# A hybrid encoder trunk on one core: the first projections of layer 0 rebuilt (value projection in the loop over input tiles, shift and scale side by side, one sine chain for all angles)

## The chip, the core and the metric

The kernel runs on 1 core of one Trainium2 chip. The metric is device time in microseconds. Three runs of the kernel before took 1063.59 to 1066.42 us; the median is 1063.81 us. The core has a matrix engine (TensorE, PE in the profile; its weight loads are PEld), a vector engine (VectorE, DVE), a scalar engine (ScalarE, ACT), GpSimd (POOL) and SyncE (SP), which issues the DMA transfers of this kernel. Each engine works through its own list of instructions in order; waits between engines go by semaphores.

## The reference, cut to what matters

Two layers, 256 tokens, 1024 channels. Only the first sub-layer of layer 0 is touched, so only its head is shown.

```
cond = silu(c)
for l in range(2):
    mod = cond @ w_ada[l] + b_ada[l]                  # 1024 -> 6 * 1024
    shift1, scale1, gate1, shift2, scale2, gate2 = split(mod, 6)
    h = layer_norm(x) * (1 + scale1) + shift1
    proj = h @ w_in[l]
    q_c, kv_c, k_r, r_q, r_k, r_v, r_g, s5_u, gates = split(proj, ...)
    #  256   128   32  256  256  512  512  512   3072  columns
    o_mla = mla(q_c, kv_c, k_r, positions, ...)       # rope: cos, sin(positions * 10000**(-i/16))
    o_ret = retention(r_q, r_k, r_v, r_g, positions, log_decay)   # rope with 32 angles,
    #                                                 log_gamma = log1p(-exp(log_decay))
    o_s5 = s5(s5_u, ...)  # step = exp(log_step); a = exp(lam_re*step) * (cos, sin)(lam_im*step);
    #                       x_t = a x_(t-1) + B u_t, forward and backward, 32 groups x 64 states
    x = post_norm(alpha * x + gate1 * (sigmoid(gates) merge of the three @ w_o))
    ...                                               # conv FFN with shift2, scale2, gate2
```

## The kernel before, in words

Every operation goes through a recorder: the Python code records instructions in program order (a helper on one line issues them all, so the profile shows L736 for every row, and rows are told apart by tile names). `Recorder.schedule` (line 554) then simulates the engines with a table of costs and latencies and lists the instructions anew: on each engine the ready one with the lowest number of record goes first, moved by a bias and by a small random jitter with a fixed seed, if the pool has a place for its tiles. The pools are 37 places of 128x1024 f32 (weights, x, h and most other tiles), 9 and 18 smaller ones, and 8 banks of PSUM.

Weights come as tiles `raw` of 512 KB in the order of `_plan`, DMAs on SyncE. Each is split into `hi` (a cast to fp32r on ACT) and `lo` (raw minus hi, on DVE), and a product is three matmuls: hi with the activation's high part hh, lo with hh, and hi with the activation's low part hlo. Activations h are kept transposed, 8 tiles of 128 channels by 256 tokens.

`mixer` (line 1422) computes layer 0's first sub-layer. Its first part is a loop over k = 0, 2, 4, 6, two channel tiles a round. A round has: `ada_chunk` for the chunk of shift1 and then that of scale1 which belong to these 256 channels (each: two loads `ada0`, 8 matmuls 32x256 into a PSUM tile ada_ps, a copy z, two transposes, a reduction and an addition on DVE); `put_h`, which transposes the normalised x and applies scale and shift; `gemm_t` for b0 (q_c, kv_c and k_r, 416 columns) and for b1 (r_q and r_k, 512 columns), both accumulating in PSUM over all four rounds. The tile names b0, b1, b2 are one group "b" in the profile.

Behind the loop `rope_tables` (line 979) makes the cosine and sine of 352 columns in one chain of DVE instructions (`sincos`, line 924; tiles t): 96 columns for two token tiles (tokens on partitions), and 256 for the table qtab, whose angles stand on partitions and come from posf_i, the positions loaded to all 128 partitions. `prephase` (line 997) makes exp(log_step) and exp(log_decay) (tiles arena), the decays lg and nlg (16 columns, some 45 instructions), a second `sincos` of 64 columns, the powers pw, the factors fri, and by seven squarings the steps rot8. Then `s5.prep` (bbt) and `s5.rot` (tiles rot and g) build the tables of the S5 stage. kr is the first product of k_r with a rope table, and so the first use of the finished b0. uF is the S5 input; it is transposed in 32x32 blocks into uT0 and by two copies into uT.

b2 (r_v, 512 columns, 48 matmuls) is computed after the up-projection `ukv` of the latent. Then the S5 stage follows: `states` transposes tables into w_ps (tile w1), DVE makes scans X, results R are written to DRAM (rd) and read back as T, and PE multiplies T with U into Y.

Of the kernel before, what the change touches and what calls it, by code (L numbers as in the profile page):

```python
# [18 lines left out]
L = 2  # L19
# [47 lines left out]
def _plan(layer):  # L67
# [28 lines left out]
    if layer == 0:  # L96
        for k in range(0, 8, 2):
            block_t("b0_", "w_in", 0, 416, 2, [k])
            block_t("b1_", "w_in", 416, 928, 2, [k])
        block_f("u", "w_in", 1952, 4)  # L100
    else:
        block_t("b0_", "w_in", 0, 416, 2)
        block_f("u", "w_in", 1952, 4)
        block_t("b1_", "w_in", 416, 928, 2)
    for g in range(2):
        out.append((f"uq{g}", 1024, lambda w, l, g=g: uq(w, l, g)))
    out.append(("ukv", 1024, ukv))
    block_t("b2_", "w_in", 928, 1440, 2)
    names = ("w_branch_mla", "w_branch_ret", "w_branch_s5")
# [39 lines left out]

def ada_rows(l, c):  # L150

    return (l, c // 4) not in ((0, 0), (0, 1))


def _ada(w, l, key):
    c, k = (int(v) for v in key[3:].split("_"))
    if ada_rows(l, c):
        k += 2 * (c % 4)
        return w["w_ada"][l][k * P:(k + 1) * P, c // 4 * D:(c // 4 + 1) * D]
    return _rows(w["w_ada"][l][k * 512:(k + 1) * 512, c * 256:(c + 1) * 256]).reshape(P, -1)  # L160

# [22 lines left out]
def _small_layout():  # L184
    off, o = {}, 0
    for name, n in (("c", 8), ("lam_re", 64), ("lam_im", 64), ("log_step", 64), ("ret_ld", 16),
                    ("kv_norm", L), ("q_norm", 2 * L), ("conv_w", L * NFF * 2 * 3), ("conv_b", L * NFF * 2),
                    ("b_ada", L * 32), ("d", L * 8), ("freq_t", 48), ("freq_f", 1), ("sign_f", 1),
                    ("i16", 16)):
        off[name] = (o, o + n)  # L190
        o += n
    return off, o


def _host(w):
# [34 lines left out]
    put("freq_t", np.broadcast_to(np.concatenate([fr, fm])[None], (P, 48)))  # L230
    put("freq_f", np.concatenate([np.zeros(64, f32), fm, fm, fm, fm]))
    put("sign_f", np.concatenate([np.ones(96, f32), -np.ones(16, f32), np.ones(16, f32)]))
    i16 = np.tile(np.concatenate([np.eye(16, dtype=f32), np.zeros((16, 16), f32)]), (4, 1))
    put("i16", i16)

    def bc(a):
# [12 lines left out]
        "x": w["x"].reshape(2, P, D),  # L249
        "pos": w["positions"].reshape(1, S),  # L250
        "post": w["positions"].reshape(2, P).T,
# [488 lines left out]
def build(tc, A, dbg=None):  # L740
# [237 lines left out]

    def rope_tables():
        w = []  # L980
        for i in range(5):
            w2 = t4([P, 1024], f"t{i}")
            w += [w2[:, 0:352], w2[:, 512:864]]
        ang, sn, cs = w[6:9]
# [12 lines left out]
    def prephase():  # L997
        main[0] = V if PRE0 == 'V' else G

        ex = pre(80)  # L1000
        exi = pre(80)
        V.tensor_copy(exi[:, 0:64], sm("log_step"))
        V.tensor_copy(exi[:, 64:80], sm("ret_ld"))
        exp_acc(ex, exi, 80)
        step = ex[:, 0:64]
        e = ex[:, 64:80]

        q = [pre(16) for i in range(9)]
        y1, kx, m1, sel, nsel, num, den, z_, z2 = q
        ts(y1, e, -1.0, ALU.mult, 1.0, ALU.add)  # L1010
# [28 lines left out]

        main[0] = PRE[0]  # L1040
# [5 lines left out]
        main[0] = PRE[1]  # L1046

# [27 lines left out]
        for n in (1, 2, 4):  # L1075
# [3 lines left out]
                 br, bi, pt[0][:, :, 0:n], pt[1][:, :, 0:n])  # L1079
        main[0] = PRE[2]  # L1080
        V.tensor_copy(w[0], c_s)
        V.tensor_copy(w[1], s_s)
        for i in range(7):
            tt(w[2], w[0], w[0], ALU.mult)
            tt(w[3], w[1], w[1], ALU.mult)
            tt(w[4], w[0], w[1], ALU.mult)
            dst = (w[0], w[1]) if i < 2 else (rot8[:, i - 2, 0], rot8[:, i - 2, 1])
            if i >= 2:
                tt(dst[0], w[2], w[3], ALU.subtract)
                ts(dst[1], w[4], 2.0, ALU.mult)  # L1090
                V.tensor_copy(w[0], dst[0])
                V.tensor_copy(w[1], dst[1])
            else:
                tt(w[0], w[2], w[3], ALU.subtract)
                ts(w[1], w[4], 2.0, ALU.mult)
# [59 lines left out]

    def ada_chunk(l, c, kind=None):
        if ada_rows(l, c):
            return ada_part(l, c, kind)
        sec, sub = SEC[c // 4], c % 4
# [9 lines left out]
        AC.copy(z, ps[:, 0:256])
        for b in range(2):  # L1170
            T.transpose(ps[:, 256 + b * P:256 + (b + 1) * P], z[:, b * P:(b + 1) * P], ident)
        m = modc[l, sec][:, 2 * sub:2 * sub + 2]
        V.tensor_reduce(out=m, in_=ps[:, 256:512].rearrange("p (b c d) -> p b c d", b=2, d=32)[:, :, :, 0],
                        op=ALU.add, axis=AX.X)
        ib = ("shift1", "scale1", "shift2", "scale2").index(sec)
        bcol = sm("b_ada", l * 32 + ib * 8 + 2 * sub, l * 32 + ib * 8 + 2 * sub + 2)
        if sec.startswith("scale"):
            stt(m, m, 1.0, ALU.add, bcol, ALU.add)
        else:
            tt(m, m, bcol, ALU.add)  # L1180

# [240 lines left out]
    def mixer(l, xt, h, s5, xdram, ready=None, pre_=None):  # L1422
# [134 lines left out]

        ps2 = banks("b2")
        for k in range(0, 8, 2):
            gemm_t(need(l, f"b2_{k}"), h, 512, k, ps2, k == 0, k == 6)  # L1560
        rv = t4([P, 1024], "rv")
        for t in range(2):
            evac(rv[:, t * 512:(t + 1) * 512], ps2[t])

# [415 lines left out]
```

## Time and profile before

| | |
|---|---|
| median of three runs | 1063.81 us (1063.59 to 1066.42) |
| profiled execution | 1065.51 us, span 1063.7 us, 20435 instructions |
| PE busy | 991.2 us (93%), 8080 matmuls; PEld 848.8 us (80%) |
| DVE busy | 855.2 us (80%), 1729 instructions |
| ACT busy | 480.3 us (45%); POOL 31.6 us (3%) |
| moved by DMA | 214.19 MB, mean 201 GB/s |

Busy shares are means over a span with stages of different limits: the first 13 us have no matmul, the loop that follows is full of DMA, and later stages are full of PE or DVE. So the prediction reads stretches, not the means. In rows of a list of instructions a first number is the start in us, the second how long the row's instructions took together, and xN at the end says how many instructions the row holds. DVE and PE begin an instruction before the listed duration of the last one is over, so a distance between starts is shorter than a listed duration.

### The profile page before, as it was taken

To read this page: it belongs to the slowest core of one execution; us is meant where nothing else is said; L and a number is where in the kernel's file an instruction comes from. 1 tells how busy PE (TensorE), PEld (TensorE's weight loads), DVE (VectorE), ACT (ScalarE), POOL (GpSimd) and SP (SyncE) were. 2 spreads that over 40 slices of the span, in tenths; PEclk is the share of its full clock that TensorE was granted. 3 is DMA by queue.
4 is the path that set the end of the run, shared out by engine and by line. 5 is a ranking of instruction groups with operands and counts; after the bars stand their busy time and mean duration, and the time that the engine had idled before them with its cause. 6 is when DMAs were issued, how large, how long until landed. Compare 5 with 4: busy or idle time off the path is not lost.

```text
span 1063.7 us, 20435 instructions
## 1 busy us (share of the span) xinstructions
PE 991.2 (93%) x8080; PEld 848.8 (80%) x8080; DVE 855.2 (80%) x1729; ACT 480.3 (45%) x857; POOL 31.6 (3%) x43
## 2 busy tenths in 40 slices
PE   4877999997999999999998999998799979999996
PEld 2557875776898689999985988786689869999995
DVE  7999999881659998777889997998175899777766
ACT  2352353121464556655543645321155466555640
POOL 0000000000000100000001000000000010000001
PEclk9888999998999999999998999999899989999998
DMA  8962335446887787555549721733688546555600
GB/s 339 408 236 101 121 99 203 135 135 193 323 311 268 281 309 232 177 190 182 185 134 361 279 96 59 262 116 117 187 314 297 197 137 218 198 184 191 216 25 39
DMA packets 67456, 214.19 MB, mean 201 GB/s; under 512 B 7824, under 2 KB 16160, under 8 KB 67360
## 3 DMA queue, kind: packets, MB, share of 16 engines
q1 hardware_dynamic: 67360, 212.88, 56.8%
q8 instruction: 63, 1.03, 0.4%
q14 instruction: 33, 0.27, 0.1%
HBM read 209.76 MB, written 3.10 MB: 200 GB/s over the span
## 4 chain that ended last, share of the span: by engine, by line
PE 77%; DVE 14%; DMA 5%; issue 1%; ACT 1%; SPq 0%; POOL 0%; POOLq 0%; DVEq 0%; ACTq 0%
PE up_ps L736 22%; PE g_ps L736 13%; PE dn_acc L736 11%; PE br_ps L736 5%; PE b L736 5%; PE wo_acc L736 4%; DMA ada<-in_wts 3%; DVE g L736 2%; PE ada_ps L736 2%; PE upt L736 2%; DMA adab<-in_wts 1%; PE w_ps L736 1%; DVE lo L736 1%; PE St L736 1%; DVE arena L736 1%
## 5 line engine op out<-in xcount | busy, mean ns | idle before, releaser
L736 DVE TENSOR_TENSOR lo<-raw,hi 128x1024 fp32r<-128x1024 f32 (+1 forms) x210 | 251.3, 1214 | 64.0 <-PE up_ps L736 20.6
L736 ACT CAST hi<-raw 128x1024 fp32r<-128x1024 f32 (+1 forms) x210 | 214.2, 1042 | 71.8 <-PE wo_acc L736 23.5
L736 PE MATMUL up_ps<-hlo,hi 128*128 128x256 f32 x640 | 181.1, 283 | 0.0
L736 PE MATMUL up_ps<-hh,lo 128*128 128x256 f32 x640 | 181.1, 283 | 0.0
L736 PE MATMUL up_ps<-hh,hi 128*128 128x256 f32 x640 | 181.0, 283 | 0.0
L736 PEld LDWEIGHTS up_ps<-hh,hi 128*128 128x128 f32 x640 | 122.7, 192 | 1.7 <-issue 0.4
L736 PEld LDWEIGHTS up_ps<-hlo,hi 128*128 128x128 f32 x640 | 122.7, 192 | 1.2
L736 PE MATMUL g_ps<-hw,raw 128*128 128x256 f32 x512 | 123.7, 387 | 0.0
L736 PEld LDWEIGHTS up_ps<-hh,lo 128*128 128x128 f32 x640 | 122.7, 192 | 0.1
L736 PEld LDWEIGHTS g_ps<-hw,raw 128*128 128x128 f32 x512 | 94.6, 193 | 16.6 <-issue 5.6
L736 DVE SCALAR_TENSOR_TENSOR cv<-up_ps,small,cv 128x255 f32<-128x255 f32 x176 | 73.2, 476 | 14.9 <-ACT cv L736 14.7
L736 PE MATMUL dn_acc<-lo,ah 128*128 128x512 f32 x176 | 68.7, 391 | 0.0
L736 PE MATMUL dn_acc<-hi,al 128*128 128x512 f32 x176 | 67.9, 390 | 0.0
L736 PE MATMUL dn_acc<-hi,ah 128*128 128x512 f32 x176 | 66.2, 392 | 0.0
L736 ACT ACTIVATE cv<-up_ps,small 128x256 f32<-128x256 f32 x88 | 44.9, 562 | 37.4 <-PE up_ps L736 36.9
L736 ACT ACTIVATE gt<-g_ps 128x256 f32<-128x256 f32 x48 | 18.4, 383 | 85.4 <-PE g_ps L736 85.4
L736 ACT CAST hl<-raw 128x512 fp32r<-128x512 f32 x48 | 28.6, 618 | 55.1 <-DMA raw<-in_wts 21.7
L736 DVE TENSOR_TENSOR hl<-raw,hl 128x512 fp32r<-128x512 f32 x48 | 32.1, 685 | 14.6 <-ACT hl L736 14.5
L736 DVE TENSOR_TENSOR w<-g,g 128x512 f32<-128x512 f32 x64 | 43.0, 685 | 0.3
L736 DVE TENSOR_TENSOR g<-bC,pw 128x512 f32<-128x512 f32 x64 | 41.6, 681 | 1.7 <-PE rTo L736 1.5
L736 DVE TENSOR_TENSOR g<-pw,bbt 128x512 f32<-128x512 f32 x64 | 40.9, 684 | 0.0
L736 PEld LDWEIGHTS dn_acc<-hi,al 128*128 128x128 f32 x176 | 33.0, 188 | 7.3
(321 smaller groups left out, 2102.7 us busy)
## 6 DMA issues: line engine op xcount, KB each, us to landing
raw<-in_wts SPq DMA_DIRECT2D x262, 512.0 KB
ada<-in_wts SPq DMA_DIRECT2D x48, 512.0 KB
adab<-in_wts SPq DMA_DIRECT2D x48, 512.0 KB
T<-rd SPq DMA_DIRECT2D x64, 64.0 KB
lnrow<-in_rows SPq DMA_DIRECT2D x8, 512.0 KB
raw<-in_wts SPq DMA_DIRECT2D x8, 416.0 KB
x<-in_x SPq DMA_DIRECT2D x4, 512.0 KB
rows<-in_rows SPq DMA_DIRECT2D x4, 512.0 KB
```

What stands on the lines that cost most here:

```text
L736: getattr(o.eng.real, method)(*a, **kw)
```

## The change

It touches layer 0's first projections and the tables beside them, and one detail of both layers:

- b2 moves into the loop: each round has b0, b1 and b2 of its two channel tiles, and its weights stand there in the stream of loads. r_v is copied out of PSUM right behind the loop. In layer 1 b2 stays where it was.
- `ada_start` makes shift and scale of a round's two channel tiles in one PSUM tile: four loads, 32 matmuls 32x128, one copy z, one transpose, two DVE instructions. The stored order of these weights changes to fit.
- `tables` replaces `rope_tables` and the first half of `prephase`: one exp chain, then one `sincos` of 160 columns (96 of rope and 64 of S5). qtab is made from the token-major tables through a tile qb, by four small ACT instructions, two PE transposes and one ACT copy. The load posf_i goes.
- `powers` is the rest of `prephase`. A squaring is now (c+s)(c-s) and 2cs, written straight to its place, without copies. `decays` is recorded later, just before `states(0)`.
- uT is written by the transpose itself, in both layers, without uT0 and the two copies.

```diff
@@ _plan, layer 0
         for k in range(0, 8, 2):
             block_t("b0_", "w_in", 0, 416, 2, [k])
             block_t("b1_", "w_in", 416, 928, 2, [k])
+            block_t("b2_", "w_in", 928, 1440, 2, [k])
...
-    block_t("b2_", "w_in", 928, 1440, 2)
+    if layer:
+        block_t("b2_", "w_in", 928, 1440, 2)
...
-    posf_i = t4([P, 1024], "posf_i", I32)
-    SY.dma_start(out=posf_i[:, 0:S], in_=A["pos"].to_broadcast([P, S]))
...
-    def rope_tables():
...
-        V.tensor_copy(ang[:, 96:352], posf_i[:, 0:S])
-        ts(ang[:, 96:352], ang[:, 96:352], sm("freq_f"), ALU.mult)
-        sincos(sn, cs, ang, w[:6])
-        V.tensor_copy(snt, sn[:, 0:96])
-        V.tensor_copy(cst, cs[:, 0:96])
-        V.tensor_copy(qtab[0:96], cs[0:96, 96:352])
-        ts(qtab[96:128], sn[96:128, 96:352], sm("sign_f")[96:128], ALU.mult)
+    def tables():
+
+        ex, exi, ang = pre(80), pre(80), pre(160)
+        V.tensor_copy(exi[:, 0:64], sm("log_step"))
+        V.tensor_copy(exi[:, 64:80], sm("ret_ld"))
+        exp_acc(ex, exi, 80)
+        V.tensor_copy(lg, ex[:, 64:80])
+        named["step"] = ex[:, 0:64]
         post = sp.tile([P, 2], F32, name="post")
         V.tensor_copy(post, post_i)
         for t in range(2):
             ts(ang[:, t * 48:t * 48 + 48], sm("freq_t"), post[:, t:t + 1], ALU.mult)
...
+        tt(ang[:, 96:160], sm("lam_im"), ex[:, 0:64], ALU.mult)
+        sincos(snt, cst, ang, [pre(160) for _ in range(6)])
+
+        qb = t2([P, 2, 256], "qb")[:, :, 0:P]
+        co, si = (z[:, 0:96].rearrange("p (t n) -> p t n", t=2)[:, :, 32:48] for z in (cst, snt))
+        V.memset(qb[:, :, 0:64], 1.0)
+        for i in range(2):
+            act(qb[:, :, 64 + 16 * i:80 + 16 * i], co, AF.Copy)
+            act(qb[:, :, 96 + 16 * i:112 + 16 * i], si, AF.Copy, scale=(-1.0, 1.0)[i])
+        ps = bank([P, 2, P], "q_tp")
+        for t in range(2):
+            T.transpose(ps[:, t], qb[:, t], ident)
+        AC.copy(qtab, ps.rearrange("p t n -> p (t n)"))
...
-        sn, cs, ang = pre(64), pre(64), pre(64)
-        tt(ang, sm("lam_im"), step, ALU.mult)
-        sincos(sn, cs, ang, [pre(64) for _ in range(6)])
...
-        V.tensor_copy(w[0], c_s)
-        V.tensor_copy(w[1], s_s)
+        c, s_ = c_s, s_s
         for i in range(7):
-            tt(w[2], w[0], w[0], ALU.mult)
-            tt(w[3], w[1], w[1], ALU.mult)
-            tt(w[4], w[0], w[1], ALU.mult)
...
+            tt(w[4], c, s_, ALU.add)
+            tt(w[5], c, s_, ALU.subtract)
+            tt(dst[0], w[4], w[5], ALU.mult)
+            stt(dst[1], c, 2.0, ALU.mult, s_, ALU.mult)
+            c, s_ = dst
...
+    def ada_start(kp):
+
         ps = bank([P, 512], "ada_ps")
...
+        for j in range(4):
+            raw = t4([P, 1024], "ada0")
+            raw = raw_chunk(0, f"ada{2 * kp + j // 2}_{j % 2}", raw).rearrange("p (k q n) -> p k q n", k=2, q=4)
             with rec.group():
...
+                for k in range(2):
+                    for q in range(4):
+                        mm(out=ps[32 * q:32 * q + 32, 0:P], lhsT=condz[:, 2 * j + k], rhs=raw[:, k, q],
+                           start=(j + k == 0), stop=(j == 3 and k == 1))
         z = t1([P, 256], "z")
...
+        AC.copy(z[:, 0:P], ps[:, 0:P])
+        T.transpose(ps[:, P:2 * P], z[:, 0:P], ident)
+        v = ps[:, P:2 * P].rearrange("p (q d) -> p q d", d=32)[:, :, 0]
+        ks = slice(2 * kp, 2 * kp + 2)
+        tt(modc[0, "shift1"][:, ks], v[:, 0:2], sm("b_ada", 2 * kp, 2 * kp + 2), ALU.add)
+        stt(modc[0, "scale1"][:, ks], v[:, 2:4], 1.0, ALU.add, sm("b_ada", 8 + 2 * kp, 10 + 2 * kp), ALU.add)
...
@@ mixer
             h, xn = new_h(l, 1), [norm(x) for x in xt]
+            ps2 = banks("b2")
             for k in range(0, 8, 2):
-                for c in (k // 2, 4 + k // 2):
-                    ada_chunk(l, c, "ada0")
+                ada_start(k // 2)
                 for t in range(2):
                     put_h(h, l, 1, t, xn[t], [k, k + 1])
                 gemm_t(need(l, f"b0_{k}"), h, 416, k, o0, k == 0, k == 6)
                 b1(k)
-            rope_tables()
+                gemm_t(need(l, f"b2_{k}"), h, 512, k, ps2, k == 0, k == 6)
+            rv = t4([P, 1024], "rv")
+            for t in range(2):
+                evac(rv[:, t * 512:(t + 1) * 512], ps2[t])
+            tables()
             rec.bias = PRE_BIAS
-            prephase()
+            powers()
             s5.prep()
             s5.rot()
...
-        uT0 = t4([P, 4, 8, 32], "uT0")
-        V.transpose(out=uT0, in_=uF.rearrange("p m (j i) -> p m i j", i=8))
-        for g in range(2):
-            V.tensor_copy(uT[:, :, g], uT0[:, :, :, 16 * g:16 * g + 16])
+        V.transpose(out=uT.rearrange("p m g i c -> p m i g c"), in_=uF.rearrange("p m (a b i) -> p m i a b", a=2, i=8))
...
+        if l == 0:
+            decays()
         states(0)
```

The recorder's order changes with it. The rows below are instructions as they stand on an engine: operation, output from input (with the buffers' numbers), shape, and xN for so many in a row.

On DVE around the first kr, before: the powers pw and the factors fri are still being made.

```order
L736 TENSOR_TENSOR fri_700<-arena1_120 128x64
L736 TENSOR_TENSOR arena1_120<-pw_89 128x64x2
L736 TENSOR_TENSOR lo_720<-raw_358,hi_698 128x1024
L736 TENSOR_TENSOR arena2_690<-pw_89 128x64x2
L736 TENSOR_SCALAR ve_732<-ss_715 128x1
L736 TENSOR_SCALAR ve_735<-ss_715 128x1
L736 TENSOR_TENSOR pw_89<-arena1_120,arena2_690 128x64x2
L736 TENSOR_TENSOR kr_741<-b0_292,cst_423 128x16
L736 TENSOR_TENSOR kr_741<-b0_292,snt_396 128x16
```

The same place on DVE now; hh and hlo are the parts of the modulated h of the last round.

```order
L737 TENSOR_TENSOR lo_859<-raw_681,hi_844 128x1024
L737 CAST hh_672<-hw_657 128x2x128
L737 TENSOR_TENSOR hlo_678<-hw_657,hh_672 128x2x128
L737 TENSOR_TENSOR lo_881<-raw_725,hi_864 128x1024
L737 TENSOR_SCALAR ve_891<-ss_879 128x1
L737 TENSOR_TENSOR rot1_85<-g0_796,g1_805 128x32x16
L737 TENSOR_SCALAR ve_905<-ss_879 128x1
L737 TENSOR_TENSOR kr_908<-b0_309,cst_336 128x16
L737 TENSOR_TENSOR kr_908<-b0_309,snt_334 128x16 x2
```

So pw, fri, bbt and nearly all of rot now stand ahead of the first kr.

On PE at the boundary of the first and second round, before: three chunks' modulation stands between b1 and the next b0.

```order
L736 MATMUL b1_323<-hi_256,hlo_290 128x512
L736 MATMUL ada_ps_276<-ada0_147,condz_77 32x256 x4
L736 MATMUL ada_ps_276<-const_94,z_354 128x128 x2
L736 MATMUL ada_ps_365<-ada0_155,condz_77 32x256 x4
L736 MATMUL ada_ps_365<-ada0_149,condz_77 32x256 x4
L736 MATMUL ada_ps_365<-const_94,z_379 128x128 x2
L736 MATMUL ada_ps_389<-ada0_170,condz_77 32x256 x4
L736 MATMUL ada_ps_389<-ada0_183,condz_77 32x256 x4
L736 MATMUL b0_292<-hi_339,hh_285 128x416
```

The same boundary now; h_ps is the transposed x of the next round.

```order
L737 MATMUL b2_391<-lo_349,hh_302 128x512
L737 MATMUL b2_391<-hi_304,hlo_311 128x512
L737 MATMUL ada_ps_423<-ada0_144,condz_77 32x128 x8
L737 MATMUL ada_ps_423<-ada0_147,condz_77 32x128 x8
L737 MATMUL ada_ps_423<-ada0_154,condz_77 32x128 x8
L737 MATMUL ada_ps_423<-ada0_159,condz_77 32x128 x8
L737 MATMUL ada_ps_423<-const_96,z_472 128x128
L737 MATMUL h_ps_483<-const_96,xn_198 128x128 x2
L737 MATMUL ada_ps_494<-ada0_185,condz_77 32x128 x8
L737 MATMUL b0_309<-hi_363,hh_302 128x416
```

The whole modulation of round two now stands behind b2 of round one.

On SyncE around the S5 stage's way through DRAM, before: both groups of writes rd stand ahead of the next weights.

```order
L736 DMA rows<-in_rows 128x1024
L736 DMA rd_2474<-R 16x960 x4
L736 DMA T<-rd_2474 16x8x128 x16
L736 DMA rd_2729<-R 16x960 x4
L736 DMA raw<-in_wts 128x1024 x3
L736 DMA ada<-in_wts 128x1024
L736 DMA T<-rd_2729 16x8x128 x16
```

The same place now.

```order
L737 DMA rd_2450<-R 16x960 x4
L737 DMA rows<-in_rows 128x1024
L737 DMA T<-rd_2450 16x8x128 x16
L737 DMA raw<-in_wts 128x1024 x3
L737 DMA rd_2710<-R 16x960 x4
L737 DMA ada<-in_wts 128x1024 x2
L737 DMA raw<-in_wts 128x1024
L737 DMA T<-rd_2710 16x8x128 x16
```

Three loads of raw weights have moved ahead of the second group of writes.

## Rows read from the trace of the kernel before

**Rows 1.** Busy time by stage: stretch, length, engines, granted clock, DMA share, GB/s.

```profile
13.40:36.50 23.10, 18.73 (x122) 10.93 (x122) 21.00 (x67) 8.11 (x16) 0.77 (x1) 0.85 1.03 408
36.50:62.20 25.70, 24.98 (x171) 17.88 (x168) 24.91 (x150) 11.95 (x27) 2.13 (x3) 0.94 1.02 408
62.20:98.00 35.80, 23.81 (x157) 19.99 (x156) 34.75 (x130) 12.37 (x21) 1.22 (x2) 0.81 0.29 101
98.00:160.00 62.00, 61.97 (x575) 53.04 (x574) 61.55 (x114) 26.53 (x63) 0.00 (x0) 0.97 0.37 124
160.00:200.00 40.00, 39.96 (x214) 26.67 (x213) 37.70 (x78) 11.34 (x29) 1.32 (x1) 1.00 0.51 181
200.00:240.00 40.00, 36.60 (x703) 29.39 (x703) 33.07 (x77) 8.96 (x27) 1.01 (x1) 0.96 0.41 131
```

**Rows 2.** The chain of waits, 58 to 120 us: start, time, engine, tile.

```profile
94.96 0.77 DVE uT L736 x2
...
108.02 10.88 PE b L736 x48
118.90 1.20 PE w_ps L736 x11
```

**Rows 3.** Groups of DVE instructions from 62.2 to 98 us: count, busy, mean, idle.

```profile
L736 DVE TENSOR_TENSOR g<-rot,rot 128x32 f32<-128x32 f32 (+4 forms) x20 | 6.4, 365 | 0.1
...
L736 DVE TENSOR_TENSOR r<-arena 128x64 f32<-128x64 f32 x1 | 0.2, 219 | 0.0
```

**Rows 4.** DVE's instructions in order of time: start, us, operation.

```profile
23.08 0.95 DVE L736 SCALAR_TENSOR_TENSOR t<-t,t 128x352 f32<-128x352 f32 x2
23.95 0.33 DVE L736 CAST t<-t 128x352 f32<-128x352 int32 x1
24.21 0.52 DVE L736 SCALAR_TENSOR_TENSOR t<-t,t 128x352 f32<-128x352 f32 x1
...
52.53 0.19 DVE L736 TENSOR_SCALAR arena<-arena 128x64 f32<-128x64 f32 x1
...
52.77 0.50 DVE L736 TENSOR_SCALAR arena<-arena 128x64 f32<-128x64 f32 x4
...
72.98 0.49 DVE L736 TENSOR_TENSOR arena<-arena 128x64 f32<-128x64 f32 x3
...
99.43 3.49 DVE L736 TENSOR_TENSOR lo<-raw,hi 128x1024 fp32r<-128x1024 f32 x3
```

**Rows 5.** PE's matmuls in order of time, in the loop.

```profile
22.44 0.45 PE L736 MATMUL b<-hi,hh 128*128 128x416 f32 x1 [1.76 <-DVE hh L736]
...
29.19 0.64 PE L736 MATMUL ada_ps<-ada,condz 128*32 128x256 f32 x8
...
36.55 0.72 PE L736 MATMUL b<-hi,hh 128*128 128x416 f32 x1
37.07 0.55 PE L736 MATMUL b<-lo,hh 128*128 128x416 f32 x1
37.41 0.55 PE L736 MATMUL b<-hi,hlo 128*128 128x416 f32 x1
...
57.18 0.35 PE L736 MATMUL b<-lo,hh 128*128 128x416 f32 x1
57.37 0.54 PE L736 MATMUL b<-hi,hlo 128*128 128x416 f32 x2
```

**Rows 6.** DVE's instructions: the first kr and the last X of direction one.

```profile
60.20 0.17 DVE L736 TENSOR_TENSOR kr<-b,cst 128x16 f32<-128x16 f32 x1
...
137.07 0.67 DVE L736 TENSOR_TENSOR X<-va,vc 128x496 f32<-128x496 f32 x1
```

**Rows 7.** DVE's wait for the positions.

```profile
8.13 0.29 DVE L736 CAST t<-posf_i 128x256 f32<-128x256 int32 x1 [2.48 <-DMA posf_i<-in_pos]
```

**Rows 8.** PE's wait at the first Y for T.

```profile
258.94 1.08 PE L736 MATMUL Y<-T,U 128*32 128x128 f32 x16 [6.29 <-DMA T<-rd]
```

**Rows 9.** SyncE's queue: raw loads that wait for a place.

```profile
204.34 10.51 SPq L736 DMA_DIRECT2D raw<-in_wts  x2
```

More of the change, by code (lines that the diff above doesn't have):

```diff
@@ L147, in _plan, with ada_first @@
     return out
-def ada_rows(l, c):
-    return (l, c // 4) not in ((0, 0), (0, 1))
+def ada_first(l, c):
+    return l == 0 and c < 8
 def _ada(w, l, key):
     c, k = (int(v) for v in key[3:].split("_"))
[L157 to L160, printed above, removed]
+    if ada_first(l, c):
+        a = w["w_ada"][l][:, :2 * D].reshape(4, 2, P, 2, 4, 256)[2 * (c % 2) + k, :, :, :, c // 2]
+        return a.transpose(1, 0, 2, 3).reshape(P, 1024)
+    k += 2 * (c % 4)
+    return w["w_ada"][l][k * P:(k + 1) * P, c // 4 * D:(c // 4 + 1) * D]
 def _stream():
@@ L187, in _small_layout @@
                     ("kv_norm", L), ("q_norm", 2 * L), ("conv_w", L * NFF * 2 * 3), ("conv_b", L * NFF * 2),
-                    ("b_ada", L * 32), ("d", L * 8), ("freq_t", 48), ("freq_f", 1), ("sign_f", 1),
+                    ("b_ada", L * 32), ("d", L * 8), ("freq_t", 48),
                     ("i16", 16)):
@@ L230, in _host @@
     put("freq_t", np.broadcast_to(np.concatenate([fr, fm])[None], (P, 48)))
-    put("freq_f", np.concatenate([np.zeros(64, f32), fm, fm, fm, fm]))
-    put("sign_f", np.concatenate([np.ones(96, f32), -np.ones(16, f32), np.ones(16, f32)]))
     i16 = np.tile(np.concatenate([np.eye(16, dtype=f32), np.zeros((16, 16), f32)]), (4, 1))
@@ L249, in _host @@
         "x": w["x"].reshape(2, P, D),
-        "pos": w["positions"].reshape(1, S),
         "post": w["positions"].reshape(2, P).T,
@@ L871, in build @@
     mhalf = cp.tile([P, 16], F32, name="mhalf")
-    gtmp = cp.tile([P, 80], F32, name="gtmp")
+    gtmp = cp.tile([P, 144], F32, name="gtmp")
     G.memset(mhalf, -0.5)
@@ L960, in build @@
     nlg = cp.tile([P, 16], F32, name="nlg")
-    snt = cp.tile([P, 96], F32, name="snt")
-    cst = cp.tile([P, 96], F32, name="cst")
+    snt = cp.tile([P, 160], F32, name="snt")
+    cst = cp.tile([P, 160], F32, name="cst")
     qtab = cp.tile([P, S], F32, name="qtab")
@@ L977, in cmul @@
         tt(outi, t0, t1, ALU.add, eng, flex)
-    def rope_tables():
[L980 to L984, printed above, removed]
+    def tables():
[5 more added lines that the diff above has]
+        named["step"] = ex[:, 0:64]
         post = sp.tile([P, 2], F32, name="post")
@@ L988, in rope_tables, with decays @@
             ts(ang[:, t * 48:t * 48 + 48], sm("freq_t"), post[:, t:t + 1], ALU.mult)
-        V.tensor_copy(ang[:, 96:352], posf_i[:, 0:S])
-        ts(ang[:, 96:352], ang[:, 96:352], sm("freq_f"), ALU.mult)
-        sincos(sn, cs, ang, w[:6])
-        V.tensor_copy(snt, sn[:, 0:96])
-        V.tensor_copy(cst, cs[:, 0:96])
-        V.tensor_copy(qtab[0:96], cs[0:96, 96:352])
-        ts(qtab[96:128], sn[96:128, 96:352], sm("sign_f")[96:128], ALU.mult)
[L997 to L1009, printed above, removed]
+        tt(ang[:, 96:160], sm("lam_im"), ex[:, 0:64], ALU.mult)
[10 more added lines that the diff above has]
+        AC.copy(qtab, ps.rearrange("p t n -> p (t n)"))
+    def decays():
+        e = lg
+        y1, kx, m1, sel, nsel, num, den, z_, z2 = (gtmp[:, 16 * i:16 * i + 16] for i in range(9))
         ts(y1, e, -1.0, ALU.mult, 1.0, ALU.add)
@@ L1038, in prephase, with powers @@
         dump("lg", lg)
-        main[0] = PRE[0]
-        sn, cs, ang = pre(64), pre(64), pre(64)
-        tt(ang, sm("lam_im"), step, ALU.mult)
-        sincos(sn, cs, ang, [pre(64) for _ in range(6)])
-        main[0] = PRE[1]
+    def powers():
+        step, sn, cs = named["step"], snt[:, 96:160], cst[:, 96:160]
         mag = pre(64)
@@ L1079, in prephase @@
                  br, bi, pt[0][:, :, 0:n], pt[1][:, :, 0:n])
-        main[0] = PRE[2]
-        V.tensor_copy(w[0], c_s)
-        V.tensor_copy(w[1], s_s)
+        c, s_ = c_s, s_s
         for i in range(7):
-            tt(w[2], w[0], w[0], ALU.mult)
-            tt(w[3], w[1], w[1], ALU.mult)
-            tt(w[4], w[0], w[1], ALU.mult)
[L1087 to L1095, printed above, removed]
+            dst = (w[2 * (i % 2)], w[2 * (i % 2) + 1]) if i < 2 else (rot8[:, i - 2, 0], rot8[:, i - 2, 1])
+            tt(w[4], c, s_, ALU.add)
[3 more added lines that the diff above has]
+            c, s_ = dst
         tt(w[0], mag, mag, ALU.mult)
@@ L1098, in prephase @@
         tt(r8, w[0], w[0], ALU.mult)
-        main[0] = V
         dump("pw", pw.rearrange("p a b c -> p (a b c)"))
@@ L1116, in build, with ada_chunk @@
     ada_bank = {}
-    def ada_part(l, c, kind):
+    def ada_chunk(l, c, kind=None):
         sec, sub = SEC[c // 4], c % 4
@@ L1154, in ada_part @@
                 tt(m, v, bcol, ALU.add)
[L1156 to L1159, printed above, removed]
+    def ada_start(kp):
         ps = bank([P, 512], "ada_ps")
-        for j in range(2):
-            raw = t4([P, 1024], kind or "ada")
-            raw = raw_chunk(l, f"ada{c}_{j}", raw).rearrange("p (k n) -> p k n", k=4)
+        for j in range(4):
+            raw = t4([P, 1024], "ada0")
+            raw = raw_chunk(0, f"ada{2 * kp + j // 2}_{j % 2}", raw).rearrange("p (k q n) -> p k q n", k=2, q=4)
             with rec.group():
-                for k in range(4):
-                    mm(out=ps[32 * k:32 * k + 32, 0:256], lhsT=condz[:, 4 * j + k], rhs=raw[:, k],
-                       start=(j == 0), stop=(j == 1))
+                for k in range(2):
+                    for q in range(4):
+                        mm(out=ps[32 * q:32 * q + 32, 0:P], lhsT=condz[:, 2 * j + k], rhs=raw[:, k, q],
+                           start=(j + k == 0), stop=(j == 3 and k == 1))
         z = t1([P, 256], "z")
[L1169 to L1180, printed above, removed]
+        AC.copy(z[:, 0:P], ps[:, 0:P])
[4 more added lines that the diff above has]
+        stt(modc[0, "scale1"][:, ks], v[:, 2:4], 1.0, ALU.add, sm("b_ada", 8 + 2 * kp, 10 + 2 * kp), ALU.add)
     pending, pace = [], [0, 1]
@@ L1555, in mixer @@
             evac(vsb[:, t], vps[t])
[L1558 to L1563, printed above, removed]
+        if l:
+            ps2 = banks("b2")
+            for k in range(0, 8, 2):
+                gemm_t(need(l, f"b2_{k}"), h, 512, k, ps2, k == 0, k == 6)
+            rv = t4([P, 1024], "rv")
+            for t in range(2):
+                evac(rv[:, t * 512:(t + 1) * 512], ps2[t])
         ps3, rg = [], t4([P, 1024], "rg")
```

## The prediction

> **What bounds the kernel now.** I read four views of the profile, from coarse to fine. First the busy time by stage [rows 1], where the reader is to compare TensorE (PE) and VectorE (DVE) in each stretch. From 13.4 to 62.2 us runs the first loop; DMA is full there (share 1.03 and 1.02, 408 GB/s), PE is idle 4.4 + 0.7 us. From 62.2 to 98 us PE is busy 23.81 of 35.8 us, so idle 12.0 us, at a granted clock of 0.81; DVE is busy 34.75 of 35.8. From 98 to 200 us both are full: PE lacks 0.07 us, DVE 2.75. Only from 200 to 240 us do both have slack (3.4 and 6.9 us).
>
> Second the chain of waits [rows 2]. It leaves DVE with the two copies into uT at 94.96 us, and from then on it is PE; the 48 matmuls of b2 stand on it for 10.88 us from 108.02 us, and the first transposes of the S5 stage follow at 118.90 us. So until about 96 us the order of things is set by DVE, and the b2 block is full-price PE time behind it.
>
> Third what DVE does between 62.2 and 98 us [rows 3]. All 25 groups add up to 44.0 us of durations for 34.75 us of busy time, since neighbours overlap (factor 0.79). 25.4 us of them, so 20.1 us of time, is table work of the constants (13 groups, from g<-rot to r<-arena, on the tiles arena, pw, rot, bbt); the rest serves the projections. Layer 0 waits here for tables that nothing in the loop had left room for.
>
> Fourth single rows, for prices [rows 4, 5]. DVE takes a new instruction before the last one's listed duration is over, so the price of one is its spacing. Two 352-wide two-input instructions start at 23.08 us and the next one at 23.95: spacing 0.43. That next one has one input and is followed at 24.21: 0.26. For 64 columns three two-input ones take 0.49 us with 0.22 of the last one's own (r<-arena, 219 ns): (0.49 - 0.22) / 2 = 0.135; four with one input take 0.50 with 0.19 of the last one's own: (0.50 - 0.19) / 3 = 0.10.
>
> **The change part by part.** The sine chain has 34 instructions in both versions: 19 with two inputs, 15 with one. Before, it runs twice, at 352 columns (19 x 0.43 + 15 x 0.26 = 12.1 us) and at 64 (19 x 0.135 + 15 x 0.10 = 4.1 us). Now it runs once at 160; on the line between the two widths one instruction costs 0.233 or 0.15, so 4.4 + 2.3 = 6.7 us. Gone: 9.5 us. With it go six helpers of 96 to 256 columns (posf_i to float, its scaling, copies into snt, cst and qtab), between 0.10 and 0.26 each: 1.1 us. The table qtab is now made by two PE transposes, four small ScalarE (ACT) instructions and one copy; ACT is busy only 11.95 of 25.7 us in that stretch [rows 1], so I cost that at nothing; without that cover it would be about 1 us.
>
> The seven squarings had 28 two-input instructions, 7 scalings and 12 copies (3.8 + 0.7 + 1.2 = 5.7 us) and now have 28 two-input ones: gone 1.9 us. The modulation had 16 small DVE instructions, now 8; each is below the 0.10 of a 64-wide one: gone 0.7 us. The two uT copies go: 0.7 us [rows 2]. New are a memset and a copy of lg: 0.2 us. Sum for DVE: 9.5 + 1.1 + 1.9 + 0.7 + 0.7 - 0.2 = 13.7 us less work.
>
> On PE the change is nearly neutral. b2 moves and costs the same 48 spacings; 64 modulation matmuls of 256 columns become 128 of 128, and 12 transposes go. A 128-column one of these is not in the trace in that form; bounds are half of the 256-wide price (0.64 / 8 = 0.08 us [rows 5]) and the whole: from minus 1 us to plus 4 us, and I take 0, since the loop has 5 us of idle PE. On SyncE's queue the 128 KB of posf_i go and four 512 KB tiles of b2 come ahead of the loop's end: 2.1 MB at 408 GB/s is 5.1 us of DMA that was issued later, in a stretch with a DMA share of 0.37 [rows 1].
>
> **Where that falls.** The order shows all table work of rotations and powers ahead of the first kr instruction, and b2's four splits (lo) too; decays, some 45 instructions of 16 columns, is thinned out up to the first w1. So DVE's work in the loop grows by 20.1 us of moved tables and 4 x 1.16 = 4.6 us of splits (three take 3.49 us [rows 4]) and shrinks by 13.7 - 0.7 = 13.0 and by about 2 us of decays: plus 9.7 us. kr stood at 60.20 us [rows 6] and comes at about 70 us. PE says nearly the same: the loop's last matmuls ended at 62.2 us [rows 1] and get 10.9 us more work, of which its idle time takes 2 to 3, so b2 ends near 71 us. From kr to the last X of the first direction it was 137.07 - 60.20 = 76.9 us, and now 76.9 - 20.1 - 4.6 - 0.7 plus 2 of decays is 53.5. That X then comes at 123.4 us instead of 137.07, 13.7 us earlier. The loop becomes as long as DMA, DVE and PE each need; none is alone its bound.
>
> Two terms remain. DVE now waits 2.48 us for posf_i [rows 7]; the exponentials fill that, but x is next and lands about as late as before, so this is worth between 0 and 2.5 us, and I take 0.3. With the table work used up before the loop ends, DVE waits in the last round for the modulated h and for b0's last matmul; no row shows that wait, bounds are 0 and the 6 us that one round's chain leaves PE waiting (29.19 to 36.55 us less the modulation matmuls in it [rows 5]); I take 2 us. Sum: -13.7 - 0.3 + 2 = -12.0 us. The profiled execution took 1065.51 us (span 1063.7); it becomes 1053.5. The median of the three runs is 1063.81, 1.7 below the profiled one, so I predict 1052.
>
> **A rule that speaks against the change.** Rows first: after the wait at the round boundary the 416-column matmuls stand 0.34 us apart (37.07 and 37.41 us), in the last round 0.19 (57.18 and 57.37 us) [rows 5], and the granted clock of the first two stretches is 0.85 and 0.94, of 98 to 160 us 0.97 [rows 1]: part of the loop runs at 1.2 GHz, b2 where it stands now does not (10.88 / 48 = 0.227 us each [rows 2]). The Trainium skill, "TensorE: Matmul & The Clock Gate", section "HAM oscillation — how this bites in real kernels", advises to run all K tiles of an output in one go and says that a loop which waits for data at each K tile starts each one cold. By that rule this change takes a contiguous block apart and pays 48 x 0.227 x (0.34 / 0.19 - 1) = 8.6 us more for b2. The trace agrees for the first rounds' starts and disagrees for the last one, whose matmuls stand at the fast spacing. It is the fourth case below.
>
> **The rivals.** (1) Forecast, DVE's shorter work passes through: 1052, its own range 1047 to 1056. For it: from 98 to 200 us DVE lacks only 2.75 us [rows 1].
> (2) PE sets the pace, and DVE catches up later: PE's idle 12.0 us and its low clock (0.19 x 23.81 = 4.5 us) between 62.2 and 98 us go, and the loop's 4 of 5 us of idle are filled by b2: 20.5 us, 1043. For it: DVE has 9.2 us of slack between 160 and 240 us [rows 1]. Against it: it is full until 160, and PE must wait for its w1 tiles.
> (3) The gain is given back at the S5 stage's way through DRAM: PE waits 6.29 us at Y for T [rows 8]. In the new order three raw loads stand ahead of the second group of rd writes on SyncE's queue; two raw loads took 10.51 us to issue near there, since their places were not free [rows 9]. If that holds up R as well, 8 to 10 us are lost: 1061.
> (4) Slower: the loop becomes a chain of four rounds at the low clock. A round has 12 x (0.19 + 2 x 0.227) = 7.7 us of matmuls at 2.4 GHz and 13.8 us at the ratio 0.34 / 0.19; four of those and three boundaries of 7.4 us (29.19 to 36.55 us) from 22.44 us on [rows 5] end at 99.8 us, and kr, some 9 us before the end, at 91 us. The change loses from kr = 137.07 - 53.5 = 83.6 us on: 7.4 us lost, 1071. For it: the new order has the whole modulation of round two behind the first b2 block. Against it: later rounds have their modulation between the projections, and b2 of round two fills a boundary.
> (5) It does nothing: the loop's end moves by all that is saved behind it, 1064. For it: DMA is full in the loop.
>
> **How the numbers follow.** Chances: (1) 0.55, (2) 0.17, (3) 0.13, (4) 0.08, (5) 0.07. A measurement of this kernel can tell about 0.3%, 3.2 us, from no change. (1) and (2) are faster, of (3) I count 0.09 as faster and 0.04 as the same; (5) is the same but for 0.02 that fall to slower; so 0.81 faster, 0.09 same, 0.10 slower. Leaving out 2 in 10, mostly (4), (5) and the far side of (2), the range is 1042 to 1062.
>
> **What would show it.** Right: t of 352 columns is gone, one chain of 160 at about 6.7 us; the first kr near 70 us; no arena, pw or bbt rows behind it but the last rotation; PE's idle time between the loop and the S5 stage down from 12 us to a few; w1's first transposes at 97 to 101 us; the last X of the first direction near 124 us; everything behind it shifted by 10 to 14 us. Wrong: kr later than 83 us, DVE waits of more than 6 us in the loop, matmuls of b2 spaced above 0.3 us, or a wait of PE at Y well above 6.3 us.

## The result and the profile after

The changed kernel takes 1046.87 us (median of 4 runs, 1046.12 to 1049.42); beside it the kernel before took 1065.12. The ratio is 0.9833, 95% interval 0.9809 to 0.9858: 18.2 us less, where 12.0 were forecast. The span of the profiled execution went from 1063.7 to 1044.3 us.

First the busy time of the changed kernel by the stretches of [rows 1], with the one ahead of them (stretch, length, then PE, PEld, DVE, ACT, POOL, granted clock, DMA share, GB/s).

```profile
0.00:13.40 13.40, 2.19 (x20) 1.37 (x20) 8.01 (x42) 1.49 (x2) 1.61 (x9) 1.00 0.79 291
13.40:36.50 23.10, 16.80 (x162) 13.11 (x166) 23.00 (x113) 8.34 (x18) 0.00 (x0) 0.90 1.03 409
36.50:62.20 25.70, 24.52 (x237) 18.26 (x230) 24.99 (x94) 7.00 (x13) 0.62 (x1) 0.96 1.03 408
62.20:98.00 35.80, 35.66 (x273) 31.98 (x272) 34.28 (x83) 23.69 (x50) 2.57 (x4) 1.00 0.45 168
98.00:160.00 62.00, 61.92 (x556) 44.32 (x555) 60.62 (x123) 27.83 (x72) 0.00 (x0) 1.00 0.47 161
160.00:200.00 40.00, 36.49 (x476) 29.44 (x475) 39.07 (x89) 8.90 (x22) 2.64 (x2) 1.00 0.38 128
```

The row from 62.2 us is the one to see. From 62.2 to 98 us PE was busy 23.81 of 35.8 us at a clock of 0.81 [rows 1]; now it is busy 35.66 at 1.00. In PE time at full clock (busy time times granted clock, an estimate from these rows) that is 19.3 before and 35.7 now, 16.4 us more. The loop itself hardly gained: the two rows from 13.4 to 62.2 us give 39.4 before and 38.7 now, and 2.2 us of matmuls now stand ahead of 13.4 us. In all PE has done 17.8 us more work by 98 us, and the kernel ends 18.2 us earlier.

The chain of waits (start, us, engine, tile), beside [rows 2]:

```profile
66.93 6.67 PE b L737 x29
73.60 0.87 PE cT L737 x8
74.47 5.99 PE u_ps L737 x50
...
89.77 1.09 PE U_ps L737 x8
...
96.81 0.88 PE w_ps L737 x8
...
181.37 0.27 DVE g L737
...
206.83 0.94 PE kps L737 x48
```

Two rows of the same chain in the kernel before:

```profile
201.67 0.67 DVE orl L736
...
229.61 0.94 PE kps L736 x48
```

The chain is on PE from 66.93 us; before, DVE held it until about 96 us. The first w_ps on the chain moved from 118.90 us to 96.81, by 22.1. In neither kernel does it stay on PE to the end: DVE holds most of it once more in the S5 stage, from 181.37 to 206.83 us now and from 201.67 to 229.61 us before, so the prediction's "from then on it is PE" is true only up to 201.67 us. The end of that DVE part moved by 22.8 us.

DVE in order of time (start, us, operation), beside [rows 4] and [rows 6]:

```profile
21.97 1.02 DVE L737 SCALAR_TENSOR_TENSOR arena<-arena 128x160 f32<-128x160 f32 x4
...
23.45 0.39 DVE L737 TENSOR_SCALAR arena<-arena 128x160 f32<-128x160 f32 x2
...
44.06 0.23 DVE L737 TENSOR_TENSOR rot<-arena 128x64 f32<-128x64 f32 x1
...
69.32 0.17 DVE L737 TENSOR_TENSOR kr<-b,cst 128x16 f32<-128x16 f32 x1
...
119.36 1.26 DVE L737 TENSOR_TENSOR X<-va,vc 128x496 f32<-128x496 f32 x2
```

Four two-input instructions of 160 columns take 1.02 us with 0.32 of the last one's own, so 0.233 each, and one-input ones 0.15: the prices taken for the sine chain. The tile arena of the tables is last read at 44.06 us (before at 77.63). The first kr comes at 69.32 us, forecast near 70, and the last X of the first direction begins at about 120.0 us, forecast 123.4.

### The profile page after: what moved, and what is told of

The parts are those of the page before. It is cut to its first block, busy times and chain, and to the rows that moved or that the text cites. A ratio compares the mean times of both kernels' runs of the same rounds, so it can differ in the third digit from the quotient of the medians.

```text
span 1044.3 us, 20597 instructions
## 1 busy us (share of the span) xinstructions
PE 983.1 (94%) x8198; PEld 847.3 (81%) x8198; DVE 841.2 (81%) x1658; ACT 481.7 (46%) x860; POOL 32.0 (3%) x43
## 4 chain that ended last, share of the span: by engine, by line
PE 79%; DVE 12%; DMA 4%; SPq 2%; issue 1%; ACT 1%; POOLq 0%; POOL 0%; DVEq 0%; ACTq 0%
PE up_ps L737 22%; PE g_ps L737 12%; PE dn_acc L737 11%; PE b L737 5%; PE br_ps L737 5%; PE wo_acc L737 3%; PE ada_ps L737 3%; PE upt L737 3%; DVE g L737 2%; PE u_ps L737 2%; SPq L737 2%; DVE arena L737 2%; DMA ada<-in_wts 2%; PE St L737 1%; PE w_ps L737 1%
## 5 line engine op out<-in xcount | busy, mean ns | idle before, releaser
L737 PE MATMUL ada_ps<-ada,condz 128*32 128x128 f32 (+1 forms) x512 | 29.6, 354 | 11.2 <-DMA ada<-in_wts 11.1
```

The costliest lines, as they stand in the source:

```text
L737: getattr(o.eng.real, method)(*a, **kw)
```

## The experiments

Times are medians; each stands beside 13 to 17 runs of the kernel before that were measured with it (medians 1064.7 to 1065.8 us). A difference between two of these kernels, worked out from their ratios, is uncertain by some 3 to 4 us. The edits are whole parts of the change put back, unless a diff shows something new.

**b2 late again.** In the changed kernel the plan line and the code of b2 stand where they stood before.

```diff
-            block_t("b2_", "w_in", 928, 1440, 2, [k])
...
-                gemm_t(need(l, f"b2_{k}"), h, 512, k, ps2, k == 0, k == 6)
...
-        if l:
-            ps2 = banks("b2")
+        ps2 = banks("b2")
```

> The changed kernel with one part undone: b2's weights and matmuls stand behind the up-projection of the latent again, as before. Theory 1 (DVE's work up to the last X sets the pace, and b2's place costs nothing by itself): the four splits are the same work on either side of kr, so the last X of direction one stays near 120 us and the time within 3 us of 1047: 1044 to 1050. Theory 2 (PE sets the pace, and b2 fills its idle time and lifts its clock in the loop): PE's 12 us of idle time between the loop and the S5 stage come back and 10.9 us of b2 stand on the path again: 1056 to 1060.

Measured: 1047.64 us, ratio 0.9832 (0.9807 to 0.9858), the same as the whole change. The row of its stretch from 62.2 us:

```profile
62.20:98.00 35.80, 35.19 (x256) 31.41 (x254) 35.45 (x75) 18.32 (x31) 0.00 (x0) 1.00 0.48 163
```

PE is full there without b2 in the loop: the first kr comes at 56.65 us, other projections follow, and b2 is one more thing that PE can do. b2's place is worth nothing that these runs can tell (0.8 us), and theory 2 in the form "b2 fills the gap" falls.

**The tables of before.**

```diff
-            tables()
+            rope_tables()
             rec.bias = PRE_BIAS
-            powers()
+            prephase()
```

> The changed kernel with the tables of before: two sine chains (352 and 64 columns), posf_i loaded, qtab by DVE, squarings with copies, decays behind the first exponentials; b2 stays in the loop, shift and scale side by side. Theory 1 (DVE's work): 12.3 us of DVE work return ahead of the last X (9.5 + 1.1 + 1.9 - 0.2), so 1059, with the wait for posf_i up to 1062. Theory 2 (PE's fill by b2 carries the gain): PE keeps its work in the loop, 1047 to 1051.

Measured: 1059.31 us, 0.9937 (0.9912 to 0.9961), 12.4 above the changed kernel, as theory 1 said. Its rows: busy time, PE's wait at u_ps, SyncE's waits for arena between 62 and 73 us (us in all, times, longest), and arena's last reader.

```profile
62.20:98.00 35.80, 28.66 (x205) 24.36 (x197) 34.56 (x125) 19.32 (x39) 2.72 (x4) 0.90 0.47 163
```

```profile
80.21 0.58 PE L740 MATMUL u_ps<-hh,hi 128*128 128x256 f32 x1 [4.46 <-ACT hi L740]
```

```profile
SPq L740 <- DVE arena L740: 5.2, 2, 5.0
```

```profile
79.91 0.22 DVE L740 TENSOR_TENSOR r<-arena 128x64 f32<-128x64 f32 x1
```

PE lacks 7.1 us here and the clock is 0.90. 4.46 us of it is a wait for ACT's cast of the first weights of u. SyncE's queue had stood 5.0 us on a reader of arena, because the tables' tiles, read here until 79.91 us, hold places of 512 KB that the next weights want. But that is not what PE waited for: the load that stood landed at 72.0 us, and ACT made the cast only at 79.11, without idle time between, behind the copies of r_v (rv) and ten instructions that make qch and kall. In the changed kernel the cast stands ahead of rv. ACT's rows, first here, then in the changed kernel:

```profile
73.88 1.07 ACT L740 COPY rv<-b 128x512 f32<-128x512 f32 x2 [3.25 <-PE b L740]
...
78.01 1.08 ACT L740 ACTIVATE kall<-cT 64x512 f32<-64x512 f32 x2
79.11 4.84 ACT L740 CAST hi<-raw 128x1024 fp32r<-128x1024 f32 x5
```

```profile
69.60 1.04 ACT L737 CAST hi<-raw 128x1024 fp32r<-128x1024 f32 x1
72.95 1.27 ACT L737 COPY rv<-b 128x512 f32<-128x512 f32 x2 [2.31 <-PE b L737]
```

So with the old tables DVE's work returns and the recorder's order on ACT changes too. The time fits theory 1, but it does not show that DVE's time is the whole cost.

**The modulation by chunks.**

```diff
-                ada_start(k // 2)
+                for c in (k // 2, 4 + k // 2):
+                    ada_chunk(l, c, "ada0")
```

> The changed kernel with the modulation of before: two chunks a round, each with its own copy, two transposes and two DVE instructions. Theory 1: 0.7 us more DVE work, 1047 to 1048. Theory 2: two waits of PE for z and the modulation in each round instead of one, some 1 us a round, 1047 to 1051.

Measured: 1058.49 us, 0.9931 (0.9906 to 0.9956), 11.6 above the changed kernel; both theories missed it. The first kr comes at 79.24 us, 10 us later. PE's waits from 12 to 82 us (what waited, for whom: us in all, times, longest):

```profile
PE b L735 <- DVE hh L735: 4.2, 4, 3.2
PE ada_ps L735 <- DVE mod0shift L735: 4.1, 3, 2.7
PE h_ps L735 <- DVE mod0scale L735: 2.0, 3, 1.0
PE h_ps L735 <- ACT hw L735: 1.8, 2, 0.9
PE ada_ps L735 <- ACT z L735: 1.5, 3, 0.5
```

These 13.6 us of waits go round from the modulation through h and back: chunk, copy, chunk, copy, transposes, matmuls. The changed kernel has 7.5 us of waits in the same stretch, and none of ada_ps for mod0shift.

**Another order of the changed kernel.** `JITTER = (18, 2)` for `(17, 2)`.

> The changed kernel with another seed of the recorder's jitter (18 for 17), the same work in a slightly different order. Theories 1 and 2: within 3 us of 1047. Rival (a good part of the 18 us is the luck of an order): it differs from 1047 by more than 4 us.

Measured: 1043.19 us, 0.9789 (0.9763 to 0.9815), by the ratios 4.7 us under the changed kernel: what the rival said, though hardly beyond the uncertainty. The order alone is thus worth some 4 us.

**Chunks and late b2 together.** Both edits above at once; what is left of the change is the tables, the powers, the decays and uT.

> The changed kernel with two parts undone together: b2 late and the modulation by chunks, as before (so: the tables, the powers, the decays and the direct uT alone). Undone singly, b2's move gave 0.8 us back and the modulation 11.6. Theory B (the modulation by chunks hurts only where b2's two accumulators leave two PSUM banks for it): 1045 to 1050. Rival (shift and scale side by side is worth 10 us by itself): 1057 to 1060.

Measured: 1048.51 us, 0.9837 (0.9816 to 0.9857). The tables' part alone has the whole gain within the uncertainty, and the chunks cost 10.0 us only with b2 in the loop (1058.49 against 1048.51; with b2 late they cost 0.9, 1047.64 against 1048.51). The parts do not add up, though: without the tables' part the others still gain 6.7 us (0.9937 above).

**Two PSUM banks held.**

```diff
+            hold = banks("hold")
+            for q in hold:
+                V.memset(q[:, 0:1], 0.0)
             for k in range(0, 8, 2):
...
+            hs = t1([P, 256], "hs")
+            V.tensor_copy(hs[:, 0:1], ps1[1][:, 0:1])
+            for i, q in enumerate(hold):
+                tt(hs[:, i + 1:i + 2], q[:, 0:1], hs[:, 0:1], ALU.add)
```

> The kernel of the run before, with two PSUM banks held by an unused tile from the start until b1 is done, so that the loop has as few banks as with b2 in it, and none of b2's work. Theory B (banks): the first kr comes 6 to 10 us later than without, 1053 to 1059. Rival (it is b2's loads, splits or matmuls in the loop that the chunks collide with): as the run without the held banks, within 3 us.

Measured: 1052.25 us, 0.9872 (0.9854 to 0.9890), 3.7 us above the run before. The first kr without and with the held banks:

```profile
57.34 0.17 DVE L733 TENSOR_TENSOR kr<-b,cst 128x16 f32<-128x16 f32 x1
```

```profile
63.38 0.26 DVE L733 TENSOR_TENSOR kr<-b,cst 128x16 f32<-128x16 f32 x2
```

kr is 6.0 us later, as theory B had it, the end less than it had, and 3.7 us are at the edge of what two such runs can tell. So banks explain at most a part of the 10 us; what b2's own work adds to it is not taken apart.

**The old uT.** The transpose into uT0 and the two copies.

> The changed kernel with the transpose into uT0 and the two copies into uT, as before. Theory 1 (DVE's work passes through): 0.77 us, 1047 to 1048.5. Rival (the order of DVE's list in the S5 stage moves with it): more than 3 us either way.

Measured: 1044.61 us, 0.9803 (0.9783 to 0.9822): not slower, and 2.3 us less is within the uncertainty. What the direct uT is worth cannot be seen in these runs.

**b2 in the loop alone**, in the kernel before.

> The kernel before with one part of the change: b2's weights, matmuls and evacuation in the loop. Theory 1 alone (b2's place costs nothing): 1062 to 1068. Theory B (banks: chunks of modulation and b2 together delay the loop by some 10 us): 1068 to 1076. Theory 2 (b2 fills PE's idle time): 1053 to 1057.

Measured: 1061.82 us, 0.9971 (0.9957 to 0.9986), 1.5 to 4.6 us gained. kr comes at 79.35 us instead of 60.20, yet the last X of the first direction at 136.59 instead of 137.07: DVE does its table work during the longer loop, so the delay costs nothing. Theory B's loss did not show.

**A wider chain.** Only the width differs:

```diff
-        sincos(snt, cst, ang, [pre(160) for _ in range(6)])
+        sincos(sn, cs, ang, wide[:6])
+        V.tensor_copy(snt, sn[:, 0:160])
+        V.tensor_copy(cst, cs[:, 0:160])
```

> The changed kernel with its one sine chain run over 352 columns instead of 160 (192 of them unused), into work tiles, and two copies of 160 columns out; everything else, loads and order of code, as changed. Theory 1 (the end moves by DVE's work ahead of the S5 stage): 19 x (0.43 - 0.233) + 15 x (0.26 - 0.153) = 5.3 us, 0.5 for the copies and a fill: 1052 to 1053.5. Rival (it is the posf_i wait, the moved decays or the order, not the width): within 2 us of 1047.

Measured: 1053.70 us (1050.51 to 1057.28), 0.9893 (0.9869 to 0.9917), 6.8 above the changed kernel. The time is about as theory 1 had it, but not the place: in the profiled execution (4.3 us longer) the last X of the first direction is 3 us late and PE's first Y<-T only 0.8. The rest comes behind the S5 stage, so this run does not prove the price.

**Idle DVE work.**

```diff
+            pad = t4([P, 1024], "pad")
+            V.memset(pad[:, 0:704], 1.0)
+            for i in range(28):
+                tt(pad[:, 0:352], pad[:, 0:352], pad[:, 352:704], ALU.mult)
```

> The changed kernel with 28 idle two-input DVE instructions of 352 columns on a tile of their own, recorded behind the tables, 28 x 0.43 = 12.0 us of DVE work that nobody waits for. Theory 1: 1057 to 1060. Rival (PE or DMA sets the pace and DVE's share only fills the loop): under 1050.

Measured: 1048.56 us, 0.9855 (0.9830 to 0.9879): 1.7 us for 12.0 us of DVE work. Theory 1 in its plain form falls. Its stretches:

```profile
0.00:13.40 13.40, 2.19 (x20) 1.37 (x20) 11.78 (x47) 1.49 (x2) 1.61 (x9) 1.00 0.82 301
...
62.20:98.00 35.80, 31.78 (x241) 28.01 (x241) 35.28 (x106) 20.78 (x43) 2.17 (x4) 1.00 0.45 164
```

3.8 us of it went into time that DVE had idle before 13.4 us (11.78 against 8.01 in the changed kernel). The last X of the first direction is 8.4 us late, but PE lacks only 4.0 us and stays at full clock.

**Two more orders.** Seed 18 in the kernel before, and in the kernel with the chunks.

> The kernel before with the jitter's seed 18 for 17. If the order's luck is worth 3 us or so either way: 1061 to 1068. If the order of before was an unlucky one: under 1060.

> The changed kernel with the modulation of before (two chunks a round) and seed 18. Theory B (with b2 in the loop the chunks lack room, whatever the order): 1052 to 1060, and the first kr some 6 to 10 us later than with shift and scale side by side. Rival (the 11.6 us were an unlucky order): 1043 to 1049.

Measured: 1066.32 us, 1.0017 (1.0001 to 1.0034), and 1053.48 us, 0.9908 (0.9879 to 0.9937). Before was no unlucky order, and b2 in the loop with the chunks is slow at either seed, as theory B had it. The chunks cost 10.3 us at this seed too (1043.19 to 1053.48), with kr at 75.72 us against 67.81.

## Why the prediction was right, and where not

**One account fits the runs.** For each kernel, PE's busy time times granted clock up to 98 us, summed over four stretches (13.4, 36.5, 62.2 and 98 us as their ends), stands beside the time. Both columns are in us and compare with the changed kernel:

| kernel | PE work missing by 98 us | time more |
|---|---|---|
| before | 17.8 | 18.2 |
| before, seed 18 | 15.0 | 19.5 |
| b2 in the loop alone | 18.8 | 15.0 |
| tables of before | 12.6 | 12.4 |
| chunks | 7.3 | 11.6 |
| chunks, seed 18 | 5.9 | 6.6 |
| two banks held | 4.3 | 5.4 |
| idle DVE work | 4.2 | 1.7 |
| wider chain | 1.6 | 6.8 |
| seed 18 | 0.5 | -3.7 |
| b2 late | -0.5 | 0.8 |
| b2 late and chunks | -1.0 | 1.6 |
| old uT | -1.7 | -2.3 |

The two columns go together within about 5 us. That is the account that the runs support: the time follows how much PE gets done before the S5 stage, and DVE's tables count by what they keep from PE. The strongest sign is the pair of 12 us: the old tables' 12.3 us of DVE work cost 12.4 us, 12.0 us that nobody waits for cost 1.7.

It is a sum that fits, and no proof. No run changes PE's work ahead of 98 us and nothing else, and behind 98 us DVE is as full as PE (39.07 of 40 us from 160 to 200 us) and holds the chain for 25 us. The first column comes from one profiled execution of each kernel, the second from medians; with the spans of those executions in its place the columns go together within 6 us. And the clock is not on record for all of the first stretch: with the old uT it reads 1.00 there, while the first round's matmuls of 416 columns stand 0.35 us apart, the spacing at the lower level:

```profile
21.81 0.55 PE L737 MATMUL b<-lo,hh 128*128 128x416 f32 x1
22.16 0.55 PE L737 MATMUL b<-hi,hh 128*128 128x416 f32 x1
```

They run from 21.30 to 25.63 us, so the first column is too low by about 2 us in that row.

**Point by point.** The number lies just under the range of the forecast's own case (1047 to 1056), towards rival (2). The prices of the sine chain held (above). DVE's work fell by 14.0 us in all (855.2 to 841.2), forecast 13.7. The loop grew as forecast, with kr at 69.32 us and the loop's last matmul at 73.21 instead of about 71. The rule on K loops that start cold (the Trainium skill, "TensorE: Matmul & The Clock Gate", section "HAM oscillation — how this bites in real kernels") says that a loop which waits at each K tile starts each one cold, which would have made b2 dearer in the loop. The trace of the changed kernel agrees for the start of the first two rounds and disagrees for b2: behind the boundary only matmuls of b0 (416 columns) stand 0.35 us apart, and b2's of the second round, but for the first step, 0.23:

```profile
37.73 0.55 PE L737 MATMUL b<-lo,hh 128*128 128x416 f32 x1
38.08 0.55 PE L737 MATMUL b<-hi,hlo 128*128 128x416 f32 x1
...
49.33 0.50 PE L737 MATMUL b<-lo,hh 128*128 128x512 f32 x1 [0.40 <-DVE lo L737]
49.67 0.40 PE L737 MATMUL b<-hi,hlo 128*128 128x512 f32 x1
49.90 0.39 PE L737 MATMUL b<-lo,hh 128*128 128x512 f32 x1
50.13 0.40 PE L737 MATMUL b<-hi,hlo 128*128 128x512 f32 x1
```

**The step that failed** is the one from "Where that falls" to the sum: that the end moves by DVE's shorter work, 13.7 us, with 2 us of a new stall taken off. The last X did come earlier, by 17.1 us. Up to the last X of the first direction DVE is busy 112.83 us instead of 127.56 and idle 7.8 instead of 10.2, so the two terms of stalls, forecast at plus 1.7 us together, came to minus 2.4: no new stall of DVE came. But DVE's work does not pass through as such: 12.0 us of it added cost 1.7. From 66.93 to 181.37 us the chain is on PE, and what the sum put at nothing is PE's idle 12.0 us and 4.5 us of low clock from 62.2 to 98 us. Rival (2) had just these two terms, 16.5 us, and the rows give 16.4. Its other term, 4 us from b2 filling the loop's gaps, was wrong: put late, b2 costs 0.8 us. That the forecast of 12.0 came as near as it did is partly luck: DVE's work fell by 14.0 us, not far from the 17.8 that PE gained.

**Given back.** Rival (3) did not come. PE's wait at Y fell from 6.29 us [rows 8] to 5.3. But a part of the gain was lost in layer 0's second half. At PE's first Y<-T the changed kernel is 21.1 us ahead (245.85 to 224.80), at the first matmul of the FFN's down projection 18.7 (386.57 to 367.86). PE's waits between 234 and 370 us, in the changed kernel and then in the kernel before:

```profile
PE Y L737 <- DMA T<-rd: 5.3, 1, 5.3
PE h_ps L737 <- ACT xn L737: 4.5, 1, 4.5
```

```profile
PE Y L736 <- DMA T<-rd: 6.3, 1, 6.3
PE upt L736 <- ACT hh L736: 2.1, 1, 2.1
PE h_ps L736 <- ACT xn L736: 0.4, 1, 0.4
```

The wait for xn is 4.1 us longer now, the one for hh that stood behind it is gone, so this place costs some 2 us. At seed 18 the two are 0.2 and 2.1 us and the down projection begins at 362.54 us, 5.3 earlier. Yet that gain does not last: the spans of the two profiled executions are 1044.0 and 1044.3 us. That of seed 18 was the slowest of its six runs, so the traces do not show where the 3.7 us between the medians come from.

**Open.** How the 12.4 us of the old tables divide between DVE's time and the order that the recorder makes around it; what besides banks makes chunks and b2 collide; where the wider chain loses behind the S5 stage; and where the two seeds differ.

## What to carry to other kernels

When two engines are full in turn, add up what the later one (here PE) gets done, clock included, by a point behind which the kernels differ little, instead of the earlier one's busy time. What a chain of small instructions costs cannot be read from its busy time: 12.3 us that others wait for cost 12.4, and 12.0 us of independent work 1.7. Parts of one change can need each other: shift and scale side by side gave 0.9 us with b2 late, but with b2 in the loop the changed kernel would have been 10 us slower without it.

## What was not expected of the hardware

Idle PE time cost more than itself where there was much of it. From 62.2 to 98 us PE lacked 12.0 us before and its clock was 0.81; with the old tables it lacked 7.1 at 0.90; with the idle DVE work 4.0 at 1.00. The sum of idle time does not tell the clock by itself, though. From 13.4 to 36.5 us PE lacked 4.5 us at 0.78 with b2 late, and 4.6 us at 1.00 with b2 late and the modulation by chunks:

```profile
13.40:36.50 23.10, 18.61 (x171) 15.06 (x172) 23.00 (x112) 8.78 (x19) 0.00 (x0) 0.78 1.03 409
```

```profile
13.40:36.50 23.10, 18.47 (x140) 11.70 (x133) 22.96 (x112) 9.95 (x22) 0.00 (x0) 1.00 1.03 409
```

A load in SyncE's queue waits for the last reader of the tile whose place it takes, and the loads behind it wait too: 5.0 us on arena with the old tables, and no load was issued from 62.79 to 67.83 us. The order on ACT can hold weights that have landed: with the old tables the first weights of u came 6 us later on PE (80.21 against 74.23 us), behind other work of ACT.
